# One of four weight sums per group made by an adding DMA, and ten more seven-product groups, in a one-core layer kernel

## The chip, the core and the metric

The kernel runs on one core of one Trainium2 chip. The metric is the device time in microseconds (us) of one execution. Three runs of the kernel before gave 1849.49, 1849.53 and 1849.77 us.

## What is computed

One layer of a streaming encoder on 256 rows (SEQ) of width 2048 (D_MODEL), all float32. Two SwiGLU feed-forward stages (FFN1 and FFN2, inner width 5632) stand around a mixer, and a per-layer embedding ends it. Cut to what matters here:

```python
def swiglu(h, w_gate, w_up, w_down):
    return (jax.nn.silu(h @ w_gate) * (h @ w_up)) @ w_down

x = x + 0.5 * swiglu(rms_norm(x, ffn1_norm[i]), ffn1_w_gate[i], ffn1_w_up[i], ffn1_w_down[i])
...                                   # mixer: S5 state space model and stick-breaking attention
x = x + 0.5 * swiglu(rms_norm(x, ffn2_norm[i]), ffn2_w_gate[i], ffn2_w_up[i], ffn2_w_down[i])
...                                   # per-layer embedding
```

## The kernel before

**Products of two halves.** Every float32 matrix is used as a high part (hi) and a low part (lo = value minus hi). A product of two matrices is three matmuls on the tensor engine (PE): hi by hi, lo by hi, hi by lo. Weights come from HBM as 1 MB tiles called `raw` (four k-tiles of 128 rows by 512 columns, pool of 5 buffers). `split` makes a pair of tiles out of half a raw: ScalarE (ACT) copies the hi part (line 181, tile `whi` or `shi`) and VectorE (DVE) subtracts (line 184, `wlo` or `slo`). `weight_pair` says where a pair goes: four pairs lie in the pool of `whi`/`wlo`, and while the list `ring` names an extra pool, three of every seven pairs go to `shi`/`slo` there, so that seven pairs can be ahead of PE.

**Blocks.** A gate and up block (index f, 11 of them per FFN) makes 512 columns of the gate and the up product from 4 groups of rows (kb = 0 to 3, each four k-tiles). A down stage walks 11 groups of rows kb for each of two pairs of output blocks (n = 0 and n = 2). A group of rows against two weight tiles can be done in two ways:

- `column`: one weight tile at a time against both row tiles, 24 matmuls, so 48 for the two tiles, with 4 splits.
- `chunk`, called a seven-product group below: a 2 by 2 block product in Winograd's form, with seven products of 6 matmuls, so 42, and 7 splits. The four quarter blocks of the weights are b11, b21 (halves of the first raw) and b12, b22 (halves of the second). Four sums are made by DVE with `add` (line 502): t1 = b11 + b12, t2 = t1 + b22, t4 = t2 + b21, t3 = b12 + b22. In the down stage each such group also makes sums of its own rows (`sum_forms`: four additions at line 459 and a split).

**Where the groups are.** In FFN1 `early` is 7: blocks 0 to 6 have columns alone, block 7 has one seven-product group, blocks 8 and 10 have two and block 9 has one. In FFN2 `early` is 0: block 0 has none, odd blocks have two and even ones one. A block with two stands in the order group, columns of the gate weights, group, columns of the up weights. In a down stage `plans` writes the order out: `s0` is a seven-product group with kb 0, `c2` are the two columns with kb 2, `a5` are the columns of kb 5 to 10, first all of one weight tile and then all of the other. There are two groups in the first plan and one in the second.

**Order.** The program is written in this order, and a scheduler then sets the order on each engine, which each engine keeps. The steps put beside a block with `put_off` are spread over it: `opened` and `gated` read finished products from PSUM, line 621 adds the last products of a block to `h`, line 216 turns `h` in 32 by 32 blocks. SyncE (SP) issues the loads of `raw`; a load waits until the last split that reads its buffer is done. GpSimd (POOL) issues a few DMAs and does little else.

Of the kernel before, what the change touches and what calls it, by code (L numbers as in the profile page):

```python
# [13 lines left out]
ALU = mybir.AluOpType  # L14
# [19 lines left out]
def layer_kernel(ctx: ExitStack, tc: tile.TileContext, a: dict, shapes: dict, out: bass.AP):  # L34
    nc = tc.nc
# [27 lines left out]
    def uid(s):  # L63
        count[0] += 1
        return f"{s}_{count[0]}"
# [4 lines left out]
    def com(tag):  # L70
        return get(comp, tag, *{"sg": (1024, 1), "h": (1024, 2), "sq": (NB, 1), "mid": (2048, 1)}[tag])

    def phase(name):
        return tc.tile_pool(name=name, bufs=1, reuse_waits="tile")
# [24 lines left out]
    def step():  # L99
        for g in list(beside):  # L100
            if next(g, beside) is beside:
                beside.remove(g)

    def finish(g):
        for _ in g:
            pass
# [175 lines left out]
    ring = [None, 0]  # L282
# [10 lines left out]
    @contextmanager  # L293
    def sums_phase(name):
        with phase(name) as pool:
            ring[:] = [pool, 0]
            yield pool
            ring[0] = None

# [150 lines left out]
    def sum_forms(pool, u, kind="n"):  # L450

        sums = pool.tile([P, 2, NB], F32, tag="sum", name=uid("rows"), bufs=2)
        s = sums.rearrange("p j n -> p (j n)").rearrange("p (z j x b) -> p z j x b", z=4, j=2, b=32)
        (a11, a21), (a12, a22) = ([u[:, k : k + 2, 4 * t : 4 * t + 4] for t in range(TT)] for k in (0, 2))
        for z, (x, y, op) in enumerate((
            (a21, a22, ALU.subtract), (s[:, 0], a11, ALU.subtract),
            (a11, a21, ALU.subtract), (a12, s[:, 1], ALU.add),
        )):
            nc.vector.tensor_tensor(out=s[:, z], in0=x, in1=y, op=op)
        both = halves(kind)  # L460
        split(*both, sums.rearrange("p j n -> p (j n)").rearrange("p (z t) -> p z t", z=4))
        return both

    class Seven:
# [39 lines left out]

        def chunk(self, kb, final=()):

            raws = []
            for w, n0 in self.ws:
                raw = wp.tile([P, 4, NB], F32, tag="raw", name=uid("raw"), bufs=5)
                nc.sync.dma_start(  # L510
                    raw, w[4 * kb * P : 4 * (kb + 1) * P, n0 : n0 + NB].rearrange("(j p) n -> p j n", p=P)
                )
                raws.append(raw)
            b11, b21, b12, b22 = (raw[:, 2 * h : 2 * h + 2, :] for raw in raws for h in range(2))
            parts, sums = self.act(kb), self.sums(kb)

            def whole(k, t):
                return [[u[:, 2 * k + j, t * P : (t + 1) * P] for j in range(2)] for u in parts]

            def summed(z):  # L520
                return [[u[:, z, j * P : (j + 1) * P] for j in range(2)] for u in sums]

            self.product(1, whole(0, 0), b11, final)
            t1 = self.add(b11, b12)
            self.product(5, summed(0), t1, final)
            step()
            t2 = self.add(t1, b22)
            self.product(6, summed(1), t2, final)
            t4 = self.add(t2, b21)
            self.product(4, whole(1, 1), t4, final)  # L530
            step()
            t3 = self.add(b12, b22)
            self.product(7, summed(2), t3, final)
            self.product(2, whole(1, 0), b21, final)
            step()
            self.product(3, summed(3), b22, final)
            step()

        def column(self, side, kbs, final=False):
# [14 lines left out]
    def ffn(i, xn, nxt, bg=None):  # L554
# [3 lines left out]
        early = 7 if bg else 0  # L558
# [19 lines left out]
        for f in range(NF):  # L578
            if prep and f == early:
                finish(prep)  # L580
                side.close()
                prep = None
                sevens = pools.enter_context(sums_phase(f"sums{i}"))
                hp = pools.enter_context(phase(f"h{i}b"))
                sums = [sum_forms(sevens, whole_rows(sevens, xn(kb)), "h") for kb in range(2)]
            if sevens and f:
                sg, hh = com("sg"), com("h")
                gate_cols, up_cols = ([u[:, t * NB : (t + 1) * NB] for t in range(TT)] for u in (sg, hh))

                def opened(s, g=gate_cols, u=up_cols):  # L590
                    nc.scalar.copy(g[0], s.bank(1))
                    nc.vector.tensor_tensor(out=u[0], in0=s.bank(6), in1=g[0], op=ALU.add)
                    nc.vector.tensor_tensor(out=u[1], in0=s.bank(7), in1=u[0], op=ALU.add)

                def gated(s, g=gate_cols, u=up_cols, hh=hh):
                    for z, (ps, other) in enumerate(((s.bank(2), g[0]), (s.bank(4), u[1]))):
                        nc.vector.tensor_tensor(out=g[z], in0=ps, in1=other, op=ALU.add)
                        nc.scalar.activation(g[z], g[z], AF.Silu, scale=xn.rs(z))
                    v = hh.rearrange("p (t n) -> p t n", t=TT)
                    nc.vector.tensor_tensor(  # L600
                        out=v, in0=s.bank(5).unsqueeze(1).to_broadcast([P, TT, NB]), in1=v, op=ALU.subtract
                    )

                s = Seven(xn, lambda kb: sums[kb], ((wg, f * NB), (wu, f * NB)), sevens)
                two = f % 2 == (0 if bg else 1)
                if f == early:
                    s.column(0, (1, 2, 3))
                    s.chunk(0, (*shared, 2, 4))
                    put_off(0, opened, s)
                elif two:  # L610
                    s.chunk(0)
                    s.column(0, (2, 3))
                    s.chunk(1, (*shared, 2, 4))
                    put_off(0, opened, s)
                else:
                    s.chunk(0, shared)
                    put_off(0, opened, s)
                    s.column(0, (1, 2, 3), True)
                put_off(0, gated, s)
                s.column(1, (2, 3) if two and f != early else (1, 2, 3), True)  # L620
                nc.vector.tensor_tensor(out=hh, in0=s.banks[3.8], in1=hh, op=ALU.add)
                for t in range(TT):
                    nc.vector.scalar_tensor_tensor(  # L623
                        out=up_cols[t], in0=up_cols[t], scalar=xn.rs(t), in1=gate_cols[t], op0=ALU.mult, op1=ALU.mult
                    )
                put_off(2, turned, hp, f, hh)
                continue

            def gate():
                for t in range(TT):  # L630
                    nc.scalar.activation(sg[:, t * NB : (t + 1) * NB], pg[t], AF.Silu, scale=xn.rs(t))

            first = ()
            if f == 0 and bg:
                warm_up(10)
                first = first_quarters(wg, xn)
            if f == 0 and not bg:
                both = gemm_pair(xn, ((wg, 0), (wu, 0)), KD)
                pg = next(both)
                sums = [sum_forms(sevens, whole_rows(sevens, xn(kb))) for kb in range(2)]  # L640
            else:
                pg = gemm_block(xn, wg, f * NB, KD, first)
            sg = com("sg")
            if f == 0 and bg:
                for n in range(ND):
                    put_off(n, load_x, n)
                    put_off(n + 2, xn.squares, n)
                put_off(6, gate)
            else:
                gate()  # L650
            pu = gemm_block(xn, wu, f * NB, KD) if f or bg else next(both)
            if prep and f == 0:
                start(prep)
            hh = com("h")
            for t in range(TT):
                nc.vector.scalar_tensor_tensor(
                    out=hh[:, t * NB : (t + 1) * NB], in0=pu[t], scalar=xn.rs(t),
                    in1=sg[:, t * NB : (t + 1) * NB], op0=ALU.mult, op1=ALU.mult,
                )
            put_off(2, turned, hp, f, hh)  # L660
# [14 lines left out]
        def opened(s, n):  # L675
# [10 lines left out]
            gather(xt[1][n + 1], one, -0.5)  # L686

        plans = (
            ("c2", "c3", "s0", "c4", "c5", "c6", "s1", "c7", "c8", "c9", "c10"),
            ("c1", "c2", "s0", "c3", "c4", "a5"),  # L690
        )
        for n in range(0, ND, 2):
            parts = {}
# [16 lines left out]
            for u in plan:  # L710
                kb, final = int(u[1:]), u == plan[-1]
# [715 lines left out]
    pool = s5p.enter_context(phase("s5"))  # L1427
# [10 lines left out]
    pool = atp.enter_context(phase("attn"))  # L1438
# [105 lines left out]
    early, part, ms, root, r, tmp = (small(1) for _ in range(6))  # L1544
# [132 lines left out]
```

## Time and profile before

| what | value |
|---|---|
| median of three runs | 1849.53 us |
| profiled execution, its own time | 1849.49 us |
| its span | 1847.7 us |
| PE busy | 1835.4 us, 99% |
| DVE busy | 1462.3 us, 79% |
| ACT busy | 1019.6 us, 55% |
| POOL busy | 62.1 us, 3% |
| HBM read | 373.46 MB |

The span runs from the first to the last instruction, and the device time has 1.8 us more. Busy shares are means over stages with unlike limits, so the table only says that PE is nearly always at work. Stages by the trace: FFN1's gate and up blocks end near 489 us, its down stage near 725, FFN2's gate and up blocks run from 1046 to 1505, its down stage to 1741. Line numbers are those of the kernel before; from line 296 on the kernel after has other numbers, at most one away in these functions.

### The profile page before, as it was taken

To read this page: it belongs to the slowest core of one execution; us is meant where nothing else is said; L and a number is where in the kernel's file an instruction comes from. 1 tells how busy PE (TensorE), PEld (TensorE's weight loads), DVE (VectorE), ACT (ScalarE), POOL (GpSimd) and SP (SyncE) were. 2 spreads that over 40 slices of the span, in tenths; PEclk is the share of its full clock that TensorE was granted. 3 is DMA by queue.
4 is the path that set the end of the run, shared out by engine and by line. 5 is a ranking of instruction groups with operands and counts; after the bars stand their busy time and mean duration, and the time that the engine had idled before them with its cause. 6 is when DMAs were issued, how large, how long until landed. Compare 5 with 4: busy or idle time off the path is not lost. (4 is left out here: it accounts for less than half of the span.)

```text
span 1847.7 us, 23966 instructions
## 1 busy us (share of the span) xinstructions
PE 1835.4 (99%) x9032; PEld 1518.1 (82%) x9032; DVE 1462.3 (79%) x1718; ACT 1019.6 (55%) x1187; POOL 62.1 (3%) x108
## 2 busy tenths in 40 slices
PE   9999999999999999999999999999999999999998
PEld 7888887788888888888898888888888888888887
DVE  8967664999987976687566799989898998797655
ACT  7444444555565655365685465555555645565554
POOL 0011000000000000010021000000000000000000
PEclk9999999999999999999999999999999999999999
DMA  9888867567656566675636776675656585656563
GB/s 331 284 270 282 251 213 220 182 227 239 229 197 241 187 233 209 192 263 166 216 139 214 219 271 212 226 240 188 205 183 228 200 267 185 247 184 232 179 220 125
DMA packets 232308, 406.36 MB, mean 220 GB/s; under 512 B 26785, under 2 KB 50721, under 8 KB 231905
## 3 DMA queue, kind: packets, MB, share of 16 engines
q1 hardware_dynamic: 227824, 392.81, 63.6%
q0 software_dynamic: 3648, 10.62, 1.8%
q8 instruction: 70, 1.15, 0.3%
q10 hardware_dynamic: 720, 1.41, 0.2%
q14 instruction: 46, 0.37, 0.1%
HBM read 373.46 MB, written 11.93 MB: 209 GB/s over the span
## 5 line engine op out<-in xcount | busy, mean ns | idle before, releaser
L184 DVE TENSOR_TENSOR wlo<-raw,whi 128x1024 fp32r<-128x1024 f32 x473 | 572.3, 1221 | 215.8 <-ACT whi L181 207.4
L181 ACT CAST whi<-raw 128x1024 fp32r<-128x1024 f32 x473 | 491.6, 1051 | 400.6 <-PE acc L324 258.0
L323 PE MATMUL acc<-whi,nhi 128*128 128x512 f32 x1112 | 436.3, 392 | 1.6 <-ACT whi L181 1.6
L324 PE MATMUL acc<-whi,nlo 128*128 128x512 f32 x1112 | 433.2, 390 | 0.0
L328 PE MATMUL acc<-wlo,nhi 128*128 128x512 f32 x1112 | 304.2, 389 | 0.3 <-DVE wlo L184 0.2
L323 PEld LDWEIGHTS acc<-whi,nhi 128*128 128x128 f32 x1112 | 209.0, 188 | 47.1 <-ACT whi L181 2.4
L328 PEld LDWEIGHTS acc<-wlo,nhi 128*128 128x128 f32 x1112 | 208.6, 188 | 44.5 <-DVE wlo L184 1.2
L324 PEld LDWEIGHTS acc<-whi,nlo 128*128 128x128 f32 x1112 | 209.1, 188 | 42.4
L184 DVE TENSOR_TENSOR slo<-raw,shi 128x1024 fp32r<-128x1024 f32 x166 | 202.0, 1217 | 42.4 <-ACT shi L181 42.3
L181 ACT CAST shi<-raw 128x1024 fp32r<-128x1024 f32 x166 | 174.3, 1051 | 110.7 <-PE acc L324 33.4
L181 ACT CAST whi<-sum 128x1024 fp32r<-128x1024 f32 x61 | 64.2, 1053 | 96.8 <-DVE sum L502 80.9
L181 ACT CAST shi<-sum 128x1024 fp32r<-128x1024 f32 x47 | 49.4, 1052 | 72.7 <-DVE sum L502 56.2
L323 PE MATMUL acc<-whi,hhi 128*128 128x512 f32 x216 | 84.1, 389 | 0.0
L324 PE MATMUL acc<-whi,hlo 128*128 128x512 f32 x216 | 84.0, 389 | 0.0
L324 PE MATMUL aux<-whi,hlo 128*128 128x512 f32 x200 | 77.9, 390 | 0.6 <-DVE hlo L184 0.6
L323 PE MATMUL aux<-whi,hhi 128*128 128x512 f32 x200 | 77.8, 389 | 0.0
L184 DVE TENSOR_TENSOR wlo<-sum,whi 128x1024 fp32r<-128x1024 f32 x61 | 74.5, 1221 | 1.9 <-ACT whi L181 1.2
L184 DVE TENSOR_TENSOR hlo<-hT,hhi 128x1024 fp32r<-128x1024 f32 x56 | 68.1, 1217 | 5.9 <-ACT hhi L181 5.7
L181 ACT CAST hhi<-hT 128x1024 fp32r<-128x1024 f32 x56 | 58.7, 1049 | 15.4 <-PE aux L328 13.1
L502 DVE TENSOR_TENSOR sum<-sum,raw 128x1024 f32<-128x1024 f32 x54 | 66.0, 1221 | 1.0
L328 PE MATMUL acc<-wlo,hhi 128*128 128x512 f32 x216 | 65.7, 390 | 0.2 <-DVE wlo L184 0.2
L323 PE MATMUL acc<-shi,hhi 128*128 128x512 f32 x160 | 62.3, 389 | 0.0
(373 smaller groups left out, 3013.7 us busy)
## 6 DMA issues: line engine op xcount, KB each, us to landing
raw<-in_ffn_w_up SPq DMA_DIRECT2D x88, 1024.0 KB, 6.0
raw<-in_ffn_w_down SPq DMA_DIRECT2D x88, 1024.0 KB, 5.1
raw<-in_ffn_w_gate SPq DMA_DIRECT2D x86, 1024.0 KB, 7.0
raw<-in_w_in SPq DMA_DIRECT2D x32, 1024.0 KB, 5.9
raw<-in_w_out SPq DMA_DIRECT2D x16, 1024.0 KB, 5.3
raw<-in_w_ple_gate SPq DMA_DIRECT2D x16, 1024.0 KB, 5.1
hT<-mid SPq DMA_DIRECT2D x160, 64.0 KB, 4.3
h<-mid SPq DMA_DIRECT2D x176, 32.0 KB, 2.7
```

The source lines that it names most:

```text
L181: copy = nc.scalar.copy(hi, src)
L184: nc.vector.tensor_tensor(out=lo, in0=src, in1=hi.bitcast(F32), op=ALU.subtract)
L323: nc.tensor.matmul(ps[t], lhsT=lh, rhs=hi[:, j, cols], start=start and j == 0, stop=False)
L324: nc.tensor.matmul(ps[t], lhsT=ll, rhs=hi[:, j, cols], start=False, stop=False)
L328: nc.tensor.matmul(ps[t], lhsT=lh, rhs=lo[:, j, cols], start=False, stop=stop and j == 1)
L502: nc.vector.tensor_tensor(out=t, in0=x, in1=y, op=ALU.add)
```

## The change

Five things are edited, all in the FFN.

- The sum t3 is no longer made by DVE. Once t1 is made, POOL issues a DMA that adds b22 onto b12 in place, from SBUF to SBUF (128 partitions of 1024 float32, 512 KB). The product with t3 (number 7) reads the second raw itself.
- t1 stands ahead of the first product, and product 7 is the last of the group, behind numbers 2 and 3.
- All blocks of FFN2 but block 0, and blocks 8 to 10 of FFN1, have two seven-product groups.
- The plans of the down stage have three and two seven-product groups, five per FFN where there were three.
- The extra pool of pairs is used from the first seven-product group of an FFN on, and no longer from the opening of the pool.

```diff
     def sums_phase(name):
         with phase(name) as pool:
-            ring[:] = [pool, 0]
             yield pool
             ring[0] = None
@@ chunk
+            if ring[0] is None:
+                ring[:] = [self.pool, 0]
             raws = []
...
+            t1 = self.add(b11, b12)
+            nc.gpsimd.dma_start(b12, b22, accum_op=ALU.add)
             self.product(1, whole(0, 0), b11, final)
-            t1 = self.add(b11, b12)
             self.product(5, summed(0), t1, final)
             step()
             t2 = self.add(t1, b22)
...
             t4 = self.add(t2, b21)
             self.product(4, whole(1, 1), t4, final)
             step()
-            t3 = self.add(b12, b22)
-            self.product(7, summed(2), t3, final)
             self.product(2, whole(1, 0), b21, final)
+            self.product(3, summed(3), b22, final)
             step()
-            self.product(3, summed(3), b22, final)
+            self.product(7, summed(2), b12, final)
             step()
@@ ffn
-                two = f % 2 == (0 if bg else 1)
+                two = f != early
...
         plans = (
-            ("c2", "c3", "s0", "c4", "c5", "c6", "s1", "c7", "c8", "c9", "c10"),
-            ("c1", "c2", "s0", "c3", "c4", "a5"),
+            ("c3", "c4", "s0", "c5", "c6", "s1", "c7", "c8", "s2", "c9", "c10"),
+            ("c2", "c3", "s0", "c4", "s1", "a5"),
         )
```

What this does to the order on the engines is shown for a block of FFN2. DVE before, one seven-product group of a block with one (raw_11414 holds b11 and b21, raw_11416 holds b12 and b22, raw_11496 belongs to the next column):

```order
L184 TENSOR_TENSOR slo_11419<-raw_11414,shi_11418 128x1024
L502 TENSOR_TENSOR sum_11428<-raw_11414,raw_11416 128x1024
L502 TENSOR_TENSOR sum_11440<-sum_11428,raw_11416 128x1024
L184 TENSOR_TENSOR wlo_11431<-sum_11428,whi_11430 128x1024
L184 TENSOR_TENSOR slo_11443<-sum_11440,shi_11442 128x1024
L502 TENSOR_TENSOR sum_11452<-sum_11440,raw_11414 128x1024
L184 TENSOR_TENSOR slo_11477<-raw_11414,shi_11476 128x1024
L502 TENSOR_TENSOR sum_11464<-raw_11416 128x1024
L184 TENSOR_TENSOR wlo_11455<-sum_11452,whi_11454 128x1024
L184 TENSOR_TENSOR slo_11499<-raw_11496,shi_11498 128x1024
L184 TENSOR_TENSOR wlo_11467<-sum_11464,whi_11466 128x1024
L184 TENSOR_TENSOR wlo_11487<-raw_11416,whi_11486 128x1024
```

DVE after, the second group of a block (raw_10835 holds b11 and b21, raw_10837 holds b12 and b22):

```order
L501 TENSOR_TENSOR sum_10839<-raw_10835,raw_10837 128x1024
L184 TENSOR_TENSOR slo_10843<-raw_10835,shi_10842 128x1024
L501 TENSOR_TENSOR sum_10862<-sum_10839,raw_10837 128x1024
L184 TENSOR_TENSOR wlo_10853<-sum_10839,whi_10852 128x1024
L184 TENSOR_TENSOR slo_10865<-sum_10862,shi_10864 128x1024
L501 TENSOR_TENSOR sum_10874<-sum_10862,raw_10835 128x1024
L184 TENSOR_TENSOR slo_10887<-raw_10835,shi_10886 128x1024
L184 TENSOR_TENSOR wlo_10877<-sum_10874,whi_10876 128x1024
L184 TENSOR_TENSOR wlo_10897<-raw_10837,whi_10896 128x1024
L184 TENSOR_TENSOR wlo_10907<-raw_10837,whi_10906 128x1024
```

The fourth sum is gone, and the last row reads the half that the DMA has added to; eight rows stand between it and the first sum. On ACT before, the casts of the same group (of raw_11414 and raw_11416) stand as:

```order
L181 CAST shi_11418<-raw_11414 128x1024
L181 CAST whi_11430<-sum_11428 128x1024
L181 CAST shi_11442<-sum_11440 128x1024
L181 CAST shi_11476<-raw_11414 128x1024
L181 CAST whi_11454<-sum_11452 128x1024
```

On ACT after, the casts of the first group of one block (raw_10679 holds b12 and b22; shi_10757 is the cast of the half that the DMA has added to):

```order
L181 CAST shi_10695<-sum_10681 128x1024
L181 CAST shi_10732<-raw_10677 128x1024
L181 CAST whi_10708<-sum_10706 128x1024
L181 CAST shi_10757<-raw_10679 128x1024
L181 CAST whi_10721<-sum_10719 128x1024
L181 CAST whi_10743<-raw_10679 128x1024
```

Here the cast that waits for the DMA stands ahead of the cast of t4 (sum_10719) and of b22; five of the 37 groups have this order, in the others it is the last cast of its group.

## The prediction

> **What bounds the kernel now.** I read the page first, then the waits of PE, then the busy times by stage, then the order in time of single engines.
>
> ```profile
> span 1847.7 us, 23966 instructions
> PE 1835.4 (99%) x9032; PEld 1518.1 (82%) x9032; DVE 1462.3 (79%) x1718; ACT 1019.6 (55%) x1187; POOL 62.1 (3%) x108
> ```
>
> PE has no work for only 12.3 us (1847.7 less 1835.4). The waits of PE say who makes it idle:
>
> ```profile
> PE acc L328 <- DVE slo L184: 2.2, 1, 2.2
> PE acc L323 <- ACT whi L181: 1.6, 2, 1.1
> ```
>
> The longest is one wait of 2.2 us, so no feeder bounds the kernel today; the number of matmuls does. What a matmul costs is read from starts in PE's order in time, six matmuls of one product:
>
> ```profile
> 1134.98 0.39 PE L495 MATMUL aux<-whi,nhi 128*128 128x512 f32 x1
> ...
> 1136.34 0.39 PE L495 MATMUL acc<-shi,hhi 128*128 128x512 f32 x1
> ```
>
> Six matmuls take 1.36 us, 0.227 us each (the duration of 0.39 overlaps the next). The second limit is seen in the busy times by stage, cut at the starts of line 621, the last addition of a block. The columns are PE, PEld, DVE, ACT, POOL:
>
> ```profile
> 489.00:605.00 116.00, 116.00 (x513) 96.08 (x512) 98.38 (x100) 65.61 (x69) 0.00 (x0) 1.00 0.61 211
> 605.00:640.00 35.00, 35.00 (x156) 28.98 (x155) 32.72 (x39) 25.33 (x34) 0.00 (x0) 1.00 0.58 184
> 640.00:665.00 25.00, 25.00 (x112) 20.71 (x111) 19.09 (x18) 12.23 (x12) 0.00 (x0) 1.00 0.72 258
> 1090.00:1505.00 415.00, 414.51 (x1826) 341.79 (x1825) 377.51 (x366) 226.73 (x237) 4.33 (x8) 1.00 0.65 218
> 1130.00:1172.00 42.00, 42.00 (x187) 34.79 (x186) 34.64 (x35) 22.16 (x24) 0.00 (x0) 1.00 0.69 226
> 1172.00:1213.00 41.00, 41.00 (x183) 33.95 (x182) 40.76 (x40) 22.59 (x24) 0.00 (x0) 1.00 0.59 205
> ```
>
> The block of FFN2 with one group (1130 to 1172) takes 42 us of PE and 34.6 of DVE; the block with two (1172 to 1213) takes 41 us of PE and 40.76 of DVE. There both engines are full. Two groups in every block with DVE's present work would have no room, so the change stands on the sum taken off DVE.
>
> **The change, part by part.** *Matmuls removed.* A group has 42 matmuls in place of 48. Groups added: one in FFN1's gate and up blocks (block 9), five in FFN2's (2, 4, 6, 8, 10), two in each down stage (5 less 3). That is 10 times 6 matmuls, 60 times 0.227 us = 13.6 us of PE's path. Nothing hides this: PE is at work for 99%, so what it doesn't do is gained, so long as it is fed.
>
> *DVE in FFN2's blocks.* The rows of one group in order of time give DVE's price:
>
> ```profile
> 1183.50 1.22 DVE L502 TENSOR_TENSOR sum<-raw,raw 128x1024 f32<-128x1024 f32 x1
> 1184.75 1.23 DVE L502 TENSOR_TENSOR sum<-sum,raw 128x1024 f32<-128x1024 f32 x1
> ...
> 1194.14 1.22 DVE L184 TENSOR_TENSOR wlo<-raw,whi 128x1024 fp32r<-128x1024 f32 x1
> 1195.28 1.22 DVE L184 TENSOR_TENSOR slo<-raw,shi 128x1024 fp32r<-128x1024 f32 x1
> ```
>
> Start to start is 1.14 us (1.25 where a sum reads the one just made). A block with two groups loses two sums: 40.76 - 2 x 1.14 = 38.5 us of DVE beside 41 of PE, 2.5 us to spare. Over the stage 1090 to 1505: five new groups add 5 x (10 - 4) operations, the fifteen old groups lose 15, so 15 x 1.14 = 17.1 us more, 394.6 of DVE against 415 - 6.8 = 408.2 of PE. It fits, at 97%. In FFN1's blocks, six operations come and six go, so there DVE stays as it is.
>
> *DVE in the down stage.* A new group costs 6 more operations there (6.8 us) and its own row sums:
>
> ```profile
> L459 DVE TENSOR_TENSOR rows<-hT x12: 414/418/426, 475.4 to 1564.1; 128x256 f32<-128x256 f32 x12
> ```
>
> Four of these at most 0.42 us and a split of 1.14 make 2.5 to 2.8 us, some 9.4 in all. The first half (489 to 605) gets 98.4 + 9.4 less two sums, 105.5 of DVE against 114.6 of PE. The start of the second half (605 to 665) gets 32.7 + 19.1 + 9.4 - 1.1 = 60.1 against 60 - 1.4 = 58.6: it is over by 1.5 us. The seven pairs ahead of PE cover that, since the long run of columns behind it (`a5`) needs little of DVE; without that cover it costs 1.5 us for each FFN, 3 in all.
>
> *The adding DMA.* No row of before shows one. Nearest are POOL's own 512 KB DMA, whose issue and landing are
>
> ```profile
> L984 POOL DMA_DIRECT2D scr_m<-m x4: 565/570/582, 149.6 to 248.7; - x4
> DMA to landing us min/median/max: 3.7/4.8/5.5
> ```
>
> and small copies within SBUF and the loads it runs beside:
>
> ```profile
> h<-mid SPq DMA_DIRECT2D x176, 32.0 KB, 2.7
> raw<-in_ffn_w_up SPq DMA_DIRECT2D x88, 1024.0 KB, 6.0
> q1 hardware_dynamic: 227824, 392.81, 63.6%
> ```
>
> Lower end: a plain copy, 4.8 us. Upper end: it fetches both operands as two full passes at the slowest landing, 2 x 5.5 = 11.0. Between: 2.7 as the fixed part and the rest, 2.1, paid twice, 6.9 us. I take 6.9, nearest to the first row, which has the same bytes and the same queue. Allowed is more: in the order of DVE after, eight rows stand between t1 and the split of the added half, 8 x 1.14 = 9.1 us from t1's end, less 1.05 for the cast ahead of it, about 8.0. Late by more than that, ACT waits with the casts of the next columns queued behind it, and DVE behind ACT. DVE's 2.5 us to spare in a block with two groups allow 1.25 us more for each, so the landing is free up to about 9.3 us. In the five groups where this cast stands ahead of that of t4, only some 3 us of casts stand between, so ACT waits about 4 us; DVE meanwhile has five splits and sums and the wait for PE at line 621, so I count it as hidden, or 5 x 4 = 20 us without that cover. By the Trainium skill's page "Collectives: The Full Stack", section "The bandwidth ceiling: the fold count and why AG ≠ RS ≠ AR", an add inside the DMA engine costs no cycles of its own, but reads two sources on the same ring and so pushes twice the read traffic of a copy. That speaks against 4.8 and for the doubled part; by it, too, the sum below stays, and no run here shows it yet.
>
> POOL itself takes 0.57 us for an issue and has 3% of the span in use; what it queues behind these, the reloads of x at the end of a gate and up stage, needs buffers that are free before the next group begins.
>
> *The extra pairs begin later.* Columns ahead of the first group now have four pairs and not seven. Places: FFN1 block 7, where PE waits already, and FFN2 block 0:
>
> ```profile
> 322.55 0.73 PE L328 MATMUL acc<-slo,nhi 128*128 128x512 f32 x2 [2.24 <-DVE slo L184]
> 1062.98 1.05 ACT L181 CAST shi<-raw 128x1024 fp32r<-128x1024 f32 x1 [9.77 <-DMA raw<-in_ffn_w_gate]
> 1066.98 0.39 PE L323 MATMUL acc<-shi,nhi 128*128 128x512 f32 x1
> ```
>
> At 1063 a load comes 9.77 us late for ACT, and PE gets to its pair at 1066.98, 1.9 us after ACT's and DVE's work on it could end (1062.98 + 1.05 + 1.1). With three pairs less ahead this margin can go. I put 2 us on each of the two places (bounds: a gain of the 2.24 that PE waits now, and three pairs of 2.7 us, 8, for either place), less 0.5 that the earlier t1 gives or takes: 3.5 us in all.
>
> *The sum.* 1849.49 (the profiled execution, 0.04 under the median) - 13.6 + 3.5 = **1839.4 us**, faster by 0.55%.
>
> **The rivals.**
>
> *A, slower: the adding DMA lands too late.* Place: the cast of the added half on ACT, 37 times. Price: above 9.3 us each microsecond is paid in every one of the 27 gate and up groups, since DVE has no more to spare there. At 11.0 us that is 1.7 x 27 = 46 us, and the time would be 1849.5 - 13.6 + 46 = 1882. It turns the sign from 13.6 / 27 = 0.5 us over, a landing near 9.8. For it: two passes are possible, and loads of 1 MB in the same queues take 6.0. Against it: 512 KB from this queue took at most 5.5. Chance 0.18.
>
> *B, about the same: DVE in its order can't use its 97%.* It waits for PE at lines 592 to 621 with the next group's splits behind, and what it loses there doesn't come back. If FFN2's blocks stay at today's 83 us for two (42 + 41) and the second halves of the down stages gain nothing, 6.8 + 2 x 1.36 = 9.5 us of the 13.6 are lost: 1845.4; with the 3.5 of the later pairs, 1848.9. For it: 40.76 of 41 us today in a block with two. Against it: in those blocks PE never waits even today. Chance 0.17, less than half of it inside 0.2%.
>
> *C, weights come late.* Adding DMAs share the sixteen engines with the loads. q1's 392.81 MB in 63.6% of 1847.7 us are 334 GB/s while busy, so an adding DMA counted as 1 MB read holds the engines for 3.1 us, 6.3 in a block with two; the DMA share rises from 0.65 to 0.80. If each of the 37 put a load back by 1 us that PE's lead doesn't cover, 37 - 13.6 makes 1873. The page "DMA: Bandwidth & Descriptors", section "Issuing engines are not separate DMA queues", of the Trainium skill says that all queues run on the same 16 engines and interleave, which is the condition for it. Against it: the share stays under 1. Chance 0.05.
>
> **How the numbers follow.** The main case has 0.60 and its own range 1835 to 1845. A difference under 0.2% (1845.8 to 1853.2) is about what a measurement of this kernel can't tell from none. Faster: the main case and 0.08 of B, 0.68. Same: 0.07 of B and a little of A, 0.08. Slower: A, C and the rest of B, 0.24. The lower end is the sum without any new wait, 1835.9, and 2 of PE's 12.3 us of idle gone, 1834; the upper end reaches into A to a landing of about 10.3 us (26 us in 27 groups, over 1835.9), 1862, which leaves out less than 2 in 10.
>
> **What would show it.** Right: 60 matmuls fewer at 0.227 us; PE idle of 12 to 18 us; the adding DMAs landing in under 8 us; DVE near 38.5 us in a block of 41 with PE busy in all of it. Wrong: waits of ACT's casts for the adding DMA of microseconds each with PE waiting for DVE behind them (A), blocks of 41.5 us with PE waiting for `wlo` or `slo` (B), or waits for `raw` (C).

## The result, and the profile after

The changed kernel takes 1835.72 us (median of 5 runs, 1833.81 to 1836.54) where the kernel before takes 1849.53 (5 runs, 1849.26 to 1849.77): a ratio of 0.9922, 95% interval 0.9909 to 0.9936, so 13.8 us faster by the medians and 0.78% by the ratio. The forecast was 1839.4. The profiled execution of the changed kernel is its fastest, 1833.81 us, 1.9 us under its median; what is read from its trace is a little on the good side.

The page's head and two of its queues, to be set beside those of before:

```profile
span 1831.7 us, 24182 instructions
...
PE 1820.2 (99%) x8972; PEld 1507.0 (82%) x8972; DVE 1506.1 (82%) x1771; ACT 1047.8 (57%) x1221; POOL 95.7 (5%) x145
...
q1 hardware_dynamic: 227824, 392.81, 64.6%
q0 software_dynamic: 8976, 30.02, 7.5%
```

PE has 60 matmuls fewer and is idle for 11.5 us (1831.7 less 1820.2), against 12.3 before: what was taken off PE was gained, and no new wait ate it. The waits of PE say which small ones changed places:

```profile
PE acc L322 <- ACT whi L181: 1.6, 2, 1.1
PE aux L494 <- ACT whi L181: 1.4, 1, 1.4
```

The 2.2 us wait for `slo` is gone, and one of 1.4 us stands in the same block. The busy times by stage (PE, PEld, DVE, ACT, POOL, then clock, DMA share and GB/s) answer the lines of before: the first half of FFN1's down stage, the start of its second half, FFN2's gate and up stage, and two of its blocks:

```profile
487.00:605.00 118.00, 118.00 (x522) 97.76 (x521) 110.40 (x114) 71.94 (x79) 2.62 (x3) 1.00 0.72 235
600.00:660.00 60.00, 60.00 (x266) 49.69 (x266) 55.36 (x62) 40.03 (x49) 1.75 (x2) 1.00 0.64 195
1083.50:1496.00 412.50, 412.38 (x1820) 341.07 (x1819) 393.54 (x382) 239.52 (x253) 20.82 (x27) 1.00 0.79 244
1166.00:1206.00 40.00, 40.00 (x178) 33.13 (x177) 39.03 (x38) 22.63 (x25) 1.73 (x2) 1.00 0.74 237
1206.00:1247.00 41.00, 41.00 (x182) 33.98 (x181) 38.58 (x39) 22.16 (x24) 1.72 (x2) 1.00 0.84 257
```

PE is full in all of them while DVE is at 92 to 98%. The adding DMA itself, line 525:

```profile
L525 POOL DMA_DIRECT2D raw<-raw x37: 847/867/907, 332.9 to 1643.3; - x37
...
  ACT shi L181: 8.4, 4
  ACT whi L181: 8.1, 4
...
DMA to landing us min/median/max: 4.5/5.7/9.6
```

Its issue takes 0.87 us of POOL, it lands after 5.7 us in the median, and in 8 of 37 groups a cast of ACT waited for it, 16.5 us in all. No long wait of PE stands behind these.

Where the time went can be dated by the last addition to x in each down stage's second half: DVE's row in order of time, of before (line 673) and of after (line 674), at the end of FFN1 and of FFN2:

```profile
724.00 1.29 DVE L673 SCALAR_TENSOR_TENSOR x<-aux,x 128x512 f32<-128x512 f32 x2 [0.86 <-PE aux L328]
1740.62 1.29 DVE L673 SCALAR_TENSOR_TENSOR x<-aux,x 128x512 f32<-128x512 f32 x2 [3.58 <-PE aux L328]
```
```profile
717.96 1.29 DVE L674 SCALAR_TENSOR_TENSOR x<-aux,x 128x512 f32<-128x512 f32 x2 [3.58 <-PE aux L327]
1723.94 1.29 DVE L674 SCALAR_TENSOR_TENSOR x<-aux,x 128x512 f32<-128x512 f32 x2 [0.86 <-PE aux L327]
```

FFN1 and its three new groups give 6.0 us (the new order of the products included); from there to the end of FFN2, with seven new groups, another 10.6.

### The profile page after: what moved, and what is told of

The parts are those of the page before. It is cut to its first block, busy times and chain, and to the rows that moved or that the text cites. A ratio compares the mean times of both kernels' runs of the same rounds, so it can differ in the third digit from the quotient of the medians.

```text
span 1831.7 us, 24182 instructions
## 1 busy us (share of the span) xinstructions
PE 1820.2 (99%) x8972; PEld 1507.0 (82%) x8972; DVE 1506.1 (82%) x1771; ACT 1047.8 (57%) x1221; POOL 95.7 (5%) x145
## 4 chain that ended last, share of the span: by engine, by line
PE 91%; DVE 5%; DMA 2%; issue 1%; ACT 1%; SPq 0%; DVEq 0%; ACTq 0%
PE acc L322 18%; PE acc L327 18%; PE acc L323 18%; PE aux L323 6%; PE aux L322 6%; PE aux L327 6%; PE acc L497 3%; PE acc L494 3%; PE acc L495 3%; PE aux L497 2%; PE aux L494 2%; PE aux L495 2%; DVE wlo L184 1%; DVE slo L184 1%; DMA raw<-in_ffn_w_down 1%
## 5 line engine op out<-in xcount | busy, mean ns | idle before, releaser
L184 DVE TENSOR_TENSOR wlo<-raw,whi 128x1024 fp32r<-128x1024 f32 x496 | 600.4, 1222 | 201.0 <-ACT whi L181 192.9
L181 ACT CAST whi<-raw 128x1024 fp32r<-128x1024 f32 x496 | 515.1, 1051 | 382.7 <-PE acc L323 256.5
L323 PE MATMUL acc<-whi,nlo 128*128 128x512 f32 x1132 | 440.8, 389 | 0.0
L501 DVE TENSOR_TENSOR sum<-sum,raw 128x1024 f32<-128x1024 f32 x74 | 90.3, 1220 | 0.5
L525 POOL DMA_DIRECT2D raw<-raw x37 | 32.1, 869 | 908.6 <-DVE sum L501 550.7
L322 PE MATMUL acc<-whi,hhi 128*128 128x512 f32 x188 | 73.1, 389 | 0.0
L323 PE MATMUL acc<-whi,hlo 128*128 128x512 f32 x188 | 73.1, 389 | 0.0
L322 PE MATMUL aux<-whi,hhi 128*128 128x512 f32 x156 | 60.7, 389 | 0.0
L323 PE MATMUL aux<-whi,hlo 128*128 128x512 f32 x156 | 60.7, 389 | 0.0
L184 DVE TENSOR_TENSOR slo<-sum,shi 128x1024 fp32r<-128x1024 f32 x46 | 56.2, 1221 | 1.2 <-ACT shi L181 0.8
```

What stands on the lines that cost most here:

```text
L181: copy = nc.scalar.copy(hi, src)
L184: nc.vector.tensor_tensor(out=lo, in0=src, in1=hi.bitcast(F32), op=ALU.subtract)
L322: nc.tensor.matmul(ps[t], lhsT=lh, rhs=hi[:, j, cols], start=start and j == 0, stop=False)
L323: nc.tensor.matmul(ps[t], lhsT=ll, rhs=hi[:, j, cols], start=False, stop=False)
L501: nc.vector.tensor_tensor(out=t, in0=x, in1=y, op=ALU.add)
L525: nc.gpsimd.dma_start(b12, b22, accum_op=ALU.add)
```

## The experiments

All are timed in five rounds beside the kernel before on the same chip; its median there was 1850.36 us for the adding DMA alone, the sum by DVE, the early pairs and the two delays, 1849.72 for the one delay, the groups in one place and the further groups, 1850.13 for the addition on POOL and the extra writes, and 1849.87 for the order alone and the repeated sum by DVE. "Over after" compares with 1835.72, which was timed beside a median of before of 1849.53; so a difference over after of 1 us or so is not settled.

**The adding DMA and the order of products alone.** The kernel before, its groups kept, with the edits inside a group: the DMA, t1 moved ahead of product 1, and product 7 moved to the end.

```diff
+            t1 = self.add(b11, b12)
+            nc.gpsimd.dma_start(b12, b22, accum_op=ALU.add)
             self.product(1, whole(0, 0), b11, final)
-            t1 = self.add(b11, b12)
...
-            t3 = self.add(b12, b22)
-            self.product(7, summed(2), t3, final)
...
+            self.product(7, summed(2), b12, final)
```

> The kernel before with the adding DMA and the new order of the products alone: its 27 groups, its plans, its ring. Theory: PE's matmuls set the time, so taking 27 sums off DVE moves nothing: 1847 to 1850, of which at most 2 us come from waits that PE has in FFN1's block 7. Rival: the room on DVE itself is the gain, by small waits of PE that go: 1840 or less. Rival A: the DMA costs waits, over 1853.

Measured: 1847.68 us, ratio 0.9988 (0.9979 to 0.9996). So 2.7 us are gained with not a matmul less.

**The order alone.** As above, without the DMA: t3 is made by DVE, just ahead of product 7 at the group's end.

```diff
+            t1 = self.add(b11, b12)
             self.product(1, whole(0, 0), b11, final)
-            t1 = self.add(b11, b12)
...
-            t3 = self.add(b12, b22)
-            self.product(7, summed(2), t3, final)
...
             step()
+            t3 = self.add(b12, b22)
+            self.product(7, summed(2), t3, final)
```

> The kernel before with the order of the products alone changed, as in the changed kernel (product 7 last in its group, its sum t3 made by DVE just ahead of it; no adding DMA, the groups of before). The adding DMA with this order, at the groups of before, brought 2.7 us against its own runs of before (1847.68 to 1850.36). Theory (that gain comes of DVE's 27 fewer sums): the order alone brings nothing, 1848.8 to 1851. Rival (it comes of the order, with which three products of loaded weights that need no sum stand last): 1846.5 to 1848.3.

Measured: 1847.12 us, ratio 0.9987 (0.9978 to 0.9996): all of the 2.7 us. The new order pays by itself (t1's move and product 7's were not run apart), and relieving DVE pays nothing while the groups are those of before. Why the order pays is not settled: the profiled run shows a wait of 0.9 us for `shi` gone from PE's list, and PE idle for 11.4 us (1846.5 less 1835.1) against 12.3; the rest is spread thin.

**The sum by DVE in the changed kernel.** Order and groups of after, t3 by DVE, no DMA.

```diff
-            nc.gpsimd.dma_start(b12, b22, accum_op=ALU.add)
...
-            self.product(7, summed(2), b12, final)
+            t3 = self.add(b12, b22)
+            self.product(7, summed(2), t3, final)
```

> The kernel after with its 37 groups, but t3 made by DVE again just ahead of product 7, no adding DMA. Theory: the sum taken off DVE is what makes room for the new groups. FFN2's gate and up stage then asks DVE for 394.6 + 20 x 1.14 = 417 us beside 408 of PE, and each down stage for 5 x 1.14 = 5.7 more, so some 9 us in FFN2's blocks, 2 in FFN1's and 1 to 3 in the down stages are lost: 1846 to 1851. Rival: DVE at 99% still keeps PE fed and the gain is the 60 matmuls alone: 1834 to 1838.

Measured: 1842.39 us, ratio 0.9958 (0.9944 to 0.9972), between the two expectations. It was run once more beside the order alone:

> The same kernel as that in which DVE makes the sum t3 in the changed kernel's order and groups, once more, beside the order alone on the same chip, so that the two are read against the same runs of before. Theory: 1842.4 again, within 1.5 us, so that the groups with DVE's present work still gain 8 us on 13.6 counted. Rival (that measurement was off by a chip's difference): outside 1841 to 1844.

Measured: 1842.51 us, ratio 0.9962 (0.9949 to 0.9976), the same. Its busy times in FFN2's gate and up stage (first run), and its longest waits of PE:

```profile
1076.00:1496.00 420.00, 416.29 (x1826) 343.15 (x1825) 415.66 (x401) 240.87 (x254) 4.35 (x8) 1.00 0.66 213
```
```profile
PE aux L494 <- ACT whi L181: 7.3, 5, 2.4
```

DVE is at work for 99% of that stage, and PE misses 3.7 of 420 us. So the relief of DVE is worth 6.7 us (1842.4 against 1835.7), or 5.8 to 6.4 when each kernel's gain over its own runs of before is compared (8.0 and 7.4 against 13.8). The ten groups would have gained 4.6 us even without it (1847.1 to 1842.5, timed together), the later start of the pairs included.

**One place of groups at a time.** The adding DMA and the order stay; new groups only in the down stages (the gate and up blocks as before), then only in the gate and up blocks (the plans as before).

```diff
-                two = f != early
+                two = f % 2 == (0 if bg else 1)
```

> The changed kernel with the gate and up groups put back to those of before (one block in two); the adding DMA and the five groups in the down stages stay. Theory (count of matmuls): 24 matmuls fewer than before, 5.4 us, and what the adding DMA alone brought, 2 us: 1841 to 1844 us. Rival (the gain lies where the ends of stages moved in the trace: 3.4 us in FFN1's down stage and 7.5 in FFN2's): 1849.5 - 10.9 = 1837 to 1840 us.

```diff
-            ("c3", "c4", "s0", "c5", "c6", "s1", "c7", "c8", "s2", "c9", "c10"),
-            ("c2", "c3", "s0", "c4", "s1", "a5"),
+            ("c2", "c3", "s0", "c4", "c5", "c6", "s1", "c7", "c8", "c9", "c10"),
+            ("c1", "c2", "s0", "c3", "c4", "a5"),
```

> The changed kernel with the down stages' plans put back to those of before (three groups per FFN); the adding DMA and the groups in nearly all gate and up blocks stay. Theory (count of matmuls): 36 fewer than before, 8.2 us, and 2 from the adding DMA: 1839 to 1842 us. Rival (the ends of stages moved by 2.6 us in FFN1's gate and up stage and by 3.4 in FFN2's, so DVE or late weights eat the rest): 1843 to 1845 us.

Measured: 1840.05 us (0.9945, 0.9933 to 0.9958) and 1838.49 us (0.9936, 0.9924 to 0.9949), 9.7 and 11.2 us under their runs of before. Less the 2.7 of the order, that is 7.0 us where 24 matmuls are 5.4, and 8.5 where 36 are 8.2: each is a little above the count of matmuls (by 1.6 and 0.3). The first lies at the rival's edge, the second below the theory's range and far from the rival's, so reading a gain from where the ends of stages moved misplaces it. That what a group saves in a gate and up block shows only later, once PE's lead is spent, would explain this; no run shows it apart. Together the groups gain 11.1 (13.8 less 2.7) where 13.6 are counted: some 2.5 us are lost, and 4.4 of the 15.5 that the two sets gain apart, only where both stand together. The runs of after spread by 1.4 us to either side of their middle, and in the fastest of them the groups gain 13.0, so how much of the loss is real stays open.

**The pairs begin as early as before.** In the changed kernel the ring of extra pairs is set where the pool opens, not at the first group.

```diff
         with phase(name) as pool:
+            ring[:] = [pool, 0]
             yield pool
...
-            if ring[0] is None:
-                ring[:] = [self.pool, 0]
```

> The kernel after with the extra pool of pairs in use from its opening, as before the change. Theory of the prediction: the later start costs 3.5 us, so undoing it gives 1831 to 1834. Rival, from the trace after, where PE waits 1.4 us in block 7 and not 2.2: the later start costs nothing, 1835 to 1838.

Measured: 1837.54 us, ratio 0.9931 (0.9919 to 0.9943), 1.8 us slower than after (1.0 by the gains over their own runs of before, 12.8 and 13.8). Its waits of PE have the old one back:

```profile
PE acc L328 <- DVE slo L184: 2.2, 1, 2.2
```

The later start costs nothing, and if it does anything it helps.

**A later landing.** Small adding DMAs of zeros on a corner of b12 are chained ahead of the large one, one or two of them.

```diff
+            for _ in range(2):      # one in the other run
+                nc.gpsimd.dma_start(b12[:, 0, :8], none, accum_op=ALU.add)
             nc.gpsimd.dma_start(b12, b22, accum_op=ALU.add)
```

With two:

> The kernel after with two adding DMAs of 128 x 8 zeros onto a corner of b12 ahead of the adding DMA, each waited for by the next, so that the sum lands some 2 x 2.5 us later, at about 11 us after t1 and not 6, with hardly more bytes. Theory A's price: landings over 9.3 us are paid in 27 groups, 1.7 x 27 = 46 us: 1875 to 1890. Rival: the pairs ahead of PE cover it and the seventh product, last in its group, isn't missed: 1835 to 1842.

Measured: 1935.31 us, ratio 1.0465 (1.045 to 1.0479), 99.6 over after. With one:

> The changed kernel with one small adding DMA of zeros (128x8) put ahead of the 512 KB one and on the same tile, so that the large one starts later. With two such DMAs the casts of the added half began some 13 to 18 us (mean about 15) after the end of the first sum t1, against about 7 in the changed kernel, and the time was 99.6 us over it. With one, I expect the casts about 11 us after t1. The prediction's limit (free up to 9.3 us, then each microsecond paid in 27 groups) gives 1.7 x 27 = 46 us over, about 1880 us. Rival: the limit lies higher, near 12 us, since PE works ahead of DVE by more than was counted; then the two delays cost (15.6 - 12) x 27 = 97 us, as measured, and one delay costs next to nothing, 1836 to 1845 us.

Measured: 1875.91 us, ratio 1.0137 (1.0123 to 1.0151), 40.2 over after. The large DMA's line in the run with one: what POOL waited for ahead of it, who waited for its landing (engine, line, us, times), and the landing itself; then those who waited in the run with two:

```profile
  DMA raw<-none: 100.2, 31
...
  ACT whi L183: 40.8, 11
  ACT shi L183: 35.7, 9
...
DMA to landing us min/median/max: 4.5/4.9/9.8
```
```profile
  ACT whi L183: 85.9, 16
  ACT shi L183: 72.4, 14
```

ACT waits 76.5 and 158.3 us for the added half, 60 and 142 more than in after, and the time rises by 40.2 and 99.6: about 0.7 us for each microsecond that ACT waits more. Not all of that is PE standing still. PE's line in the run with one delay and in that with two:

```profile
PE 1835.2 (98%) x8972; PEld 1505.7 (80%) x8972; DVE 1505.0 (80%) x1771; ACT 1043.6 (56%) x1221; POOL 128.3 (7%) x183
PE 1858.6 (96%) x8972; PEld 1520.6 (79%) x8972; DVE 1505.7 (78%) x1771; ACT 1044.6 (54%) x1221; POOL 159.5 (8%) x220
```

With spans of 1874.0 and 1933.0 us, PE is idle for 27.3 and 62.9 us more than in after, and the same 8972 matmuls keep it busy for 15.0 and 38.4 us longer; the granted clock was 0.998 and 0.984 over these runs.

How late the landing came is read group by group from the trace, from the end of t1's row to the landing. Two rows of POOL in the run with one delay show why: t1 ended at 1191.99, and the large DMA had to wait for the small one to land:

```profile
1192.63 0.87 POOL L527 DMA_DIRECT2D raw<-none  x1 [16.68 <-DVE sum L503]
1198.67 0.87 POOL L528 DMA_DIRECT2D raw<-raw  x1 [5.17 <-DMA raw<-none]
```

In after the landing comes 5.1 to 10.3 us after t1's end, median 6.4, and one of 37 is later than 9.3. With one delay it comes after 7.5 to 15.1, median 10.7, and 24 are later than 9.3; with two, after 9.9 to 18.6, median 14.4, and all are. By the forecast's rule the median of the one delay costs (10.7 - 9.3) x 27 = 38 us, and 40.2 were measured: here the limit held, and the rival that put it near 12 falls. With two, the landing was later than the 11 planned, which is why the expectation of 46 us was passed by far; the rule with the measured 14.4 gives 138, and 99.6 came. Summed over the single landings of the 27 gate and up groups, they exceed 9.3 us by 61 and 155 us, so about 0.65 us was paid for each microsecond beyond the limit, not a whole one.

**More traffic beside it.** Two plain writes of 512 KB to HBM for each group, behind the adding DMA.

```diff
             nc.gpsimd.dma_start(b12, b22, accum_op=ALU.add)
+            for spare in spares:
+                nc.gpsimd.dma_start(spare, b22)
```

> The changed kernel with two plain writes of 512 KB to HBM for each group (b22, to two scratch tiles that nobody reads), issued by POOL right behind the adding DMA: about twice 1.57 us of the sixteen engines more for each group, what the adding DMA itself takes, so the DMA share in FFN2's gate and up stage goes from 0.79 to about 0.9. Theory (the loads run far enough ahead, and the adding DMA still lands within 9.3 us): 1834 to 1840 us. Rival C of the prediction (every group's extra transfers put the loads back by 1 us or more that PE's lead doesn't cover): 37 us or more over the changed kernel, 1870 us and up. Between them: the landing gets longer by the second transfers' share, 3 us in 27 groups, less 2.7 to spare: about 1845 us.

Measured: 1852.29 us, ratio 1.0017 (1.0007 to 1.0026), 16.6 over after: the whole gain gone. The queue of POOL's transfers, FFN2's gate and up stage, and the adding DMA there:

```profile
q0 software_dynamic: 19632, 68.82, 12.7%
```
```profile
1076.00:1496.00 420.00, 414.59 (x1814) 341.90 (x1813) 391.82 (x377) 239.85 (x252) 43.77 (x68) 0.99 0.89 286
```
```profile
  ACT shi L182: 28.6, 7
  ACT whi L182: 7.0, 5
...
DMA to landing us min/median/max: 4.6/8.3/11.8
```

The landing goes from 5.7 to 8.3 us in the median, at a DMA share of 0.89, and ACT's wait for it from 16.5 to 35.6. The 19 us more cost 16.6, a little above the price of the delays (0.9 for each). The time lies above what was expected for a landing that stays in time (1834 to 1840) and far from rival C's 1870.

The writes stand behind the adding DMA in the program, but not in the order that the scheduler made for POOL, where both stand ahead of it in 31 of the 37 groups and one in the others:

```profile
1222.05 1.09 POOL L528 DMA_DIRECT2D spare<-raw  x2 [20.55 <-DMA raw<-in_ffn_w_up]
1226.01 0.89 POOL L526 DMA_DIRECT2D raw<-raw  x1 [2.87 <-DVE sum L502]
```

In 27 of the 37 groups such a write, of the same queue, had not landed when the adding DMA was issued, and there the landing took 1.8 us longer than in the same group of after (mean); in the other ten, 0.4. So this run does not show that a high share alone makes the landing late; it shows a later landing where transfers of its own queue are still under way. The loads of weights landed later too, by up to 1.0 us in the median (`in_ffn_w_gate` 7.9 to 8.9), but ACT's waits for the FFN weights stayed near what they were, 78.4 us in after and 81.7 here, so rival C's mechanism can have only a small part in the 16.6 us.

**The sum by POOL.** The same half, added in place on the engine instead of by a DMA.

```diff
-            nc.gpsimd.dma_start(b12, b22, accum_op=ALU.add)
+            nc.gpsimd.tensor_tensor(out=b12, in0=b12, in1=b22, op=ALU.add)
```

> The changed kernel with the added half b12 + b22 made in place by an addition on POOL instead of the adding DMA; order and groups as in the changed kernel. POOL's nearest rows are additions of 128x256 at 0.85 to 1.1 us, so 128x1024 should take 3.4 to 4.4 us and be done before a DMA would have landed (about 6.6 us after t1). Theory (what counts is that the sum is off DVE and ready in time): 1833 to 1837 us, as the changed kernel. Rival (POOL and DVE hold each other up while both work on SBUF, so DVE's rows beside the addition get longer, by as much as the addition's 4 us): DVE has 1.25 us to spare for each of 27 groups, (4 - 1.25) x 27 = 74 us, so 1840 to 1910 us.

Measured: 1881.36 us, ratio 1.0166 (1.0152 to 1.0181), 45.6 over after. The groups of POOL and DVE in this run, then the same two groups of DVE in after:

```profile
L525 POOL TENSOR_TENSOR raw<-raw 128x1024 f32<-128x1024 f32 x37 | 126.0, 3405 | 875.4 <-DVE sum L501 726.7 <-DMA raw<-in_ffn_w_gate 60.7 <-DMA raw<-in_ffn_w_down 49.5
L501 DVE TENSOR_TENSOR sum<-sum,raw 128x1024 f32<-128x1024 f32 x74 | 129.4, 1749 | 0.6
L184 DVE TENSOR_TENSOR slo<-sum,shi 128x1024 fp32r<-128x1024 f32 x46 | 67.9, 1476 | 0.3
```
```profile
L501 DVE TENSOR_TENSOR sum<-sum,raw 128x1024 f32<-128x1024 f32 x74 | 90.3, 1220 | 0.5
L184 DVE TENSOR_TENSOR slo<-sum,shi 128x1024 fp32r<-128x1024 f32 x46 | 56.2, 1221 | 1.2 <-ACT shi L181 0.8
```

The busy times of FFN2's gate and up stage in this run:

```profile
1076.00:1496.00 420.00, 402.74 (x1744) 324.83 (x1743) 414.85 (x365) 229.43 (x246) 60.33 (x19) 1.00 0.62 207
```

POOL is done in 3.4 us in the mean, sooner than the DMA, but the rows of DVE take 1.75 and 1.48 us in the mean of these groups in place of 1.22. The means mix two kinds of rows, as one group in order of time shows, two rows of DVE and then the addition:

```profile
1198.81 1.22 DVE L184 TENSOR_TENSOR wlo<-raw,whi 128x1024 fp32r<-128x1024 f32 x1
1199.94 3.42 DVE L501 TENSOR_TENSOR sum<-sum,raw 128x1024 f32<-128x1024 f32 x1
1199.11 3.16 POOL L525 TENSOR_TENSOR raw<-raw 128x1024 f32<-128x1024 f32 x1 [21.50 <-DVE sum L501]
```

The addition ends at 1202.27, and the row of DVE that began during it ends 1.09 us later: it stood until POOL was done and then took its usual time. In 31 of the 37 groups one row of DVE takes 3.3 to 3.4 us in this way. In two others it is POOL that stands: the addition takes 8.9 and 5.5 us while rows of DVE at 1.22 run beside it. With DVE busy for 414.85 us of 420, PE is left at 402.74. DVE's total goes from 1506.1 to 1579.8 us over the run, 2.0 for each of 37 additions, more than the 1.14 that one sum costs DVE itself, so the rival of the expectation is what happened. That the addition is off DVE's list is not enough; it has to leave DVE alone while it runs. The Trainium skill's page "SBUF — State Buffer", section "Who interferes with whom", states that a DVE instruction with two SBUF inputs contends with a GpSimd instruction that reads SBUF, and that the ports they share are an exclusive lock; the lengthened row, which has two inputs and waits for all that is left of the addition, agrees.

**Still more groups.** Two more in each FFN's down stage.

```diff
-            ("c3", "c4", "s0", "c5", "c6", "s1", "c7", "c8", "s2", "c9", "c10"),
-            ("c2", "c3", "s0", "c4", "s1", "a5"),
+            ("c4", "c5", "s0", "c6", "s1", "c7", "c8", "s2", "c9", "s3", "c10"),
+            ("s0", "c3", "s1", "c4", "s2", "a5"),
```

> The changed kernel with two more groups in each FFN's down stage (one in each half; seven per FFN instead of five), so 4 x 6 = 24 matmuls fewer, 5.4 us of PE. Theory (the prediction's count of DVE): a further group costs DVE 9.3 us. The first half had 110.4 us of DVE beside 118 of PE, and would have 119.7 beside 116.6, over by 3; the start of the second half had 54.4 beside 59, and would have 63.7 beside 57.6, over by 6. So PE waits 3 to 9 us in each FFN and the time is 1836 to 1848, no faster than the changed kernel. Rival: what PE is ahead by, and the long run of columns at the end, cover it in all stages: 1835.7 - 5.4 = 1830 us.

Measured: 1857.06 us, ratio 1.0042 (1.0028 to 1.0055), 21.3 over after with 24 matmuls fewer. The page's head, the start of the second halves in FFN1 (605 to 665) and FFN2, and the longest waits of PE:

```profile
span 1855.3 us, 24160 instructions
...
PE 1828.6 (99%) x8948; PEld 1508.0 (81%) x8948; DVE 1541.0 (83%) x1815; ACT 1061.5 (57%) x1237; POOL 97.6 (5%) x149
```

```profile
605.00:640.00 35.00, 33.51 (x141) 26.48 (x140) 33.31 (x36) 27.30 (x39) 0.84 (x1) 0.97 0.75 233
640.00:665.00 25.00, 21.97 (x82) 16.80 (x81) 23.55 (x30) 13.73 (x15) 0.85 (x1) 0.86 0.54 175
1615.00:1680.00 65.00, 56.29 (x219) 43.56 (x218) 62.23 (x70) 41.64 (x53) 2.30 (x3) 0.92 0.64 186
```
```profile
PE aux L494 <- ACT whi L181: 8.1, 4, 2.6
PE aux L494 <- ACT shi L181: 6.8, 3, 3.6
```

PE waits 1.1 and 1.9 us between 645 and 655, and 3.6, 1.5 and 2.6 us between 1615 and 1680, and there the granted clock falls, to 0.86 and 0.92: from 640 to 665 PE does 82 matmuls in 21.97 us of work, 0.268 each, where before it did 112 in 25 us, 0.223. Over the run PE is idle for 26.7 us (1855.3 less 1828.6, 15.2 more than in after), and its busy time is 8.4 us more than after's with 5.4 us of matmuls fewer: 13.8 us of slower matmuls. So a wait is paid for nearly twice here. The idle time is what was expected, 15.2 us where 3 to 9 for each FFN were named; 1857 lies above the whole range expected because that range had no slower matmuls in it. Five groups per FFN fit the down stages, and these seven don't.

No run beat the changed kernel.

## Why the prediction was right, and where its sizes were off

*Matmuls removed.* Right: 60 fewer, and PE's idle time stayed (12.3 before, 11.5 after). Of the 13.6 us counted, 11.1 came in the medians (13.8 less the 2.7 of the order).

*DVE's room.* The forecast 38.5 us of DVE in a block of 41 was 38.6, and the forecast 394.6 for FFN2's gate and up stage 393.5, beside 412.5 of PE (408.2 forecast). The start of the second half of the down stage had 55.4 of DVE in 60 us, not 60.1, and the first half 110.4 in 118 us, not 105.5: some 5 us of the work lies earlier than the count had it, and PE was full in both windows. But the sentence that the change stands on the sum taken off DVE was too strong. With the sum left on DVE the ten groups still gained 4.6 us, at 99% of DVE; the relief is worth 6 to 6.7, somewhat under half of the gain.

*The landing.* Taken as 6.9 us, bounds 4.8 to 11.0; measured 4.5 to 9.6, median 5.7. The casts that stand early in their group cost nothing that shows, as said: four of the eight waits of ACT are theirs, 2.1 to 3.2 us each where about 4 were forecast, ACT waited 16.5 us in all, and PE no longer than before. POOL's queue went from 1.8% of 1847.7 us to 7.5% of 1831.7, 104 us of all sixteen engines or 2.8 for each adding DMA (forecast 3.1); the plain writes of the same size cost 235.0 less 137.4, over 74, 1.3 each. The Trainium skill's page "Collectives: The Full Stack", section "The bandwidth ceiling: the fold count and why AG ≠ RS ≠ AR", has an add in the DMA engine read two sources, so twice the read traffic of a copy: these runs agree, 2.8 against 1.3, though the plain writes end in HBM and the adding DMA in SBUF.

*The later pairs: the step that failed.* "I put 2 us on each of the two places ... 3.5 us in all." The run with early pairs was 1.0 to 1.8 us slower instead of 3.5 faster, so this term is 0, or a small gain: its lower bound, the 2.2 us wait of PE that goes, was the right end, less the 1.4 that comes in its place.

*The order of products: the term that was missing.* The sum gave 0.5 us to the earlier t1, within the 3.5, and nothing to product 7's move to the end of its group; the two moves together are worth 2.7 us. These two errors make 1839.4 too high by 6.2, and the 2.5 us of matmuls that didn't come as gain bring it back to 3.7, the miss that was measured. So the total was nearer than its parts, by luck.

*Rival A.* Its mechanism is real: waits of ACT's casts for the added half with PE behind. Its place in after is not reached: the landing comes 6.4 us after t1's end in the median (the forecast set its 6.9, which counts from the issue, against limits that count from t1's end; 0.7 us lie between). The limit of 9.3 held where it could be tried best: a median of 10.7 us (one delay) cost 40.2, by the rule 38. The extra writes have a median of 8.9, under the limit, and cost 16.6 all the same. Thirteen of their 37 landings are later than 9.3, but only by some 10 us in all in the 27 groups, so either late landings cost before 9.3 in some groups or the writes cost in another way too; no run separates these.

*Rival B* fell: DVE can be used to 99% in its order (the sum left on DVE). *Rival C* did not appear at a share of 0.79; at 0.89 ACT's waits for the added half grew by 19 us and those for the FFN weights by 3, so the price came for the most part by A's route.

## What to carry to other kernels

Taking an operation off a full feeder pays only where the freed time is given to work that shortens the bound: 27 sums fewer gained nothing by themselves, and 37 fewer gained 6 to 6.7 us once ten more groups used the time. Move the order and the load in separate runs, since an order change that looks like a means (the product that waits for the DMA put last) can be a gain of its own. Moving work to another mover is free only in proportion to its slack: here plain writes that put 2.6 us on the median landing ended the whole gain, and each microsecond that ACT waited more cost 0.7 to 0.9.

## What the runs showed of the hardware that was not expected

An adding DMA of 512 KB within SBUF takes POOL 0.87 us to issue (0.57 for a plain transfer) and lands in 4.5 to 9.6 us; with plain writes of its own queue ahead of it, in 4.6 to 11.8. An addition on POOL makes a row of DVE that begins beside it last from 1.22 to 3.4 us, until the addition is done. Slower matmuls came with waits of PE that stand close together: after waits of 1.1 and 1.9 us that end 3.3 us apart (further groups, 649 to 652 us) the granted clock was 0.86 over 25 us, while it stayed at 1.00 in FFN2's gate and up stage of the addition on POOL, where PE was idle for 17 us in waits of up to 2.3 us spread over 420.
